# A decoder layer on one core: block 0's mixer rows beside the last projections, and four smaller moves

## The chip, the cores and the metric

One core of a Trainium2 chip. The time is that of the whole program on the device, in microseconds (us). Engines are named as in the profile: PE (tensor engine), DVE (VectorE), ACT (ScalarE), POOL (GpSimd), and SP, the queue that issues most DMAs. Each engine runs its instructions in order.

## The reference

One layer of a hybrid decoder over 2048 tokens of width 1024, one sequence, float32:

```
mod = silu(c) @ w_ada + b_ada            # shifts, scales, gates for both halves
h = rmsnorm(x, g_mix) * (1 + sc_m) + sh_m
q, k, v, f_logit, u = split(h @ w_in)    # 3 x 512, 8, 512 columns
attn = rmsnorm(forgetting_attention(q, k, v, log_sigmoid(f_logit + b)), g_attn_out)
ssm  = rmsnorm(s5_ssm(u, ...), g_ssm_out)            # 32 groups of 16 channels, 64 states
x = x + gt_m * (concat[attn, ssm] @ w_out)
h = rmsnorm(x, g_ffn) * (1 + sc_f) + sh_f
gate, val = split(h @ w_up)              # 2 x 2816 columns
y = (silu(causal_dwconv(gate, 3 taps)) * val) @ w_down
x = x + gt_f * y
out = rmsnorm(x, g_final)
```

The attention has 8 heads of 64; a score is q k / 8 plus the difference of two cumulated log gates, masked causally.

## The kernel before

**Tiles and precision.** Channels lie on the 128 partitions, tokens on the free axis; the 2048 tokens are 4 blocks of 512. Every large product is made of three matmuls in fp32r: operands are split into a high part (an ACT copy, names ending in `hi`) and the rest (a DVE subtraction, `lo`), and hi*hi, lo*hi and hi*lo are added in PSUM. A weight tile comes by DMA into `w_raw` (2 buffers) and is split into `w_hi` and `w_lo` (3 buffers each), in class `Weights`.

**Stages**, by the time of the profiled execution: to about 290 us loads, the modulation and the projection of u; to 611 the SSM, attention of block 0 and the q, k, v projections (those of blocks 2 and 3 last, they fill PE beside the SSM and attention(0)); to about 1935 the output projection and norm of block 0, attention of blocks 1 to 3 and, between its score tiles, the whole feed-forward part of blocks 0 and 1 (`up`, `down`); to 2387 the up products of blocks 2 and 3 taken in pairs (`up_pair`, 22 pairs of 19.5 us); to 2651 their down products (`down_pair`); then the last norm and the outputs.

**What sets the order.** The program is written as a list of operations; a scheduler places each engine's instructions by dependencies and priority. Code under `tc.high_priority()` goes ahead of what is written around it, `tc.issue_after(ins)` holds a DMA's place behind an instruction. A tile pool has tags with a number of buffers; a new tile of a tag waits until the readers of the tile that it replaces are done. A pool that is closed frees its memory, and later tiles at the same addresses wait in the same way.

**What the change touches.**
- `mix_t(b)` makes the operands of the output projection: it loads four row tiles of attention and SSM output (`row`, L1199 and L1200), squares the SSM half on ACT for its norm (L1202), scales it on DVE (L1208), transposes it with 16 PE transposes (L1212), scales and splits it (`yt`, `act_lo`, `act_hi`, channel tiles 4 to 7); the attention half needs its norm spread (L347) and gives channel tiles 0 to 3. `out_proj` (L1238) multiplies in the order 4, 5, 6, 7, 0, 1, 2, 3, 24 matmuls for each of 8 output tiles.
- `attention` finds row maxima of scores from augmented tiles `ka` (keys) and `qa` (queries) (L943, L948), then the scores again (L986, L987) with the maximum, the exponentials, and the products with v (L1007, L1011). Its score tiles come from `am_ps`: two PSUM banks of `att_ps` and two of a pool `sc_ps` that is opened after the projections. The augmented key tiles are three, then six.
- `ada_mid` sums a modulation gate (`tf`) on DVE beside the projections of blocks 2 and 3, from `wada` tiles that use the tags `ka3` and `ka4`; its accumulator `ada_mid` lies in the SSM's pool; the sum over partitions is a PE reading (L316).
- `finish(b)` is the last norm of block 0 or 1: token sums of squares on PE (L341), an inverse root on DVE, its spread (L347), 8 multiplications on DVE (L1311) and 8 output DMAs. For block 0 it stands at the end of that block's feed-forward part.
- `down_pair` keeps 8 output tiles in two halves of 4 PSUM accumulators; the 22 channel tiles `act` come back from DRAM in groups of 6, 6, 5 and 5 (`load_act`, one 512 KB DMA each); for each group, four weight tiles pass over it. In the last group of the last half (`cut`), two token halves p follow one another so that the first can be finished earlier; with 3 weight buffers the passes stand in the order d0 d1 d2 of p0, d0 d1 d2 of p1, then d3 of p0 and of p1. The `h` pool (9 high, 9 low tiles) holds the normed input of blocks 2 and 3 for `up_pair` and is closed before the down stage.

## Time and profile before

| | us |
|---|---|
| runs, median of three (range) | 2672.63 (2672.21 to 2674.73) |
| the profiled execution | 2669.64 |
| its span, first to last instruction | 2667.8 |
| PE busy in it | 2571.5 |
| DVE busy | 1928.8 |
| ACT busy | 1240.3 |
| POOL busy | 190.4 |
| mean granted PE clock | 0.973 |

"Busy" counts instructions of an engine on the span. A busy PE can still be slow: the granted clock says what share of its full clock it had. A window's line gives, for a stretch of the span, width, busy time and count for each engine, that clock, the DMA engines' busy share and their rate. A line of waits names who waited, for whom, the total, the number of times and the longest. In a timeline, the bracket at the end of a line holds the idle time of that engine just before, and what ended it.

### The profile page before, as it was taken

The numbers are of one execution on the slowest core, as the hardware profiler recorded it, in microseconds if no ns is written. First come the engines' busy times: TensorE is split into PE (matmuls) and PEld (weight loads), VectorE is DVE, ScalarE is ACT, GpSimd is POOL, SyncE is SP. The second block draws the span as 40 slices with busy tenths as digits, with TensorE's granted clock in tenths as the row PEclk, the third lists the DMA queues.
The fourth block names the chain that finished last, engine by engine and source line by source line (L and its number), as shares of the span: only waits on it lengthen the run. The fifth ranks groups of instructions, "written<-read, shape, count | busy, mean of one in ns | idle before, by whom it ended". The sixth has DMA issues, their size and how long they took to land. (4 is left out here: it accounts for less than half of the span.)

```text
span 2667.8 us, 35631 instructions
## 1 busy us (share of the span) xinstructions
PE 2571.5 (96%) x12343; PEld 2082.7 (78%) x12343; DVE 1928.8 (72%) x3568; ACT 1240.3 (46%) x2056; POOL 190.4 (7%) x146
## 2 busy tenths in 40 slices
...
GB/s 316 146 268 222 306 252 202 211 205 209 148 199 224 188 183 171 201 173 204 186 181 203 190 174 194 163 203 262 189 103 97 124 97 121 98 136 239 200 225 93
DMA packets 264196, 500.62 MB, mean 188 GB/s; under 512 B 26928, under 2 KB 111792, under 8 KB 264016
## 3 DMA queue, kind: packets, MB, share of 16 engines
...
q0 software_dynamic: 1280, 4.20, 0.4%
...
## 5 line engine op out<-in xcount | busy, mean ns | idle before, releaser
L78 DVE TENSOR_TENSOR w_lo<-w_raw,w_hi 128x1024 fp32r<-128x1024 f32 (+2 forms) x219 | 235.9, 1079 | 214.6 <-ACT w_hi L77 210.9
L77 ACT CAST w_hi<-w_raw 128x1024 fp32r<-128x1024 f32 (+2 forms) x219 | 203.3, 929 | 363.6 <-PE acc_ps L1481 100.9
L1264 PE MATMUL ff_ps<-h_lo,w_hi 128*128 128x512 f32 x704 | 279.3, 397 | 0.2 <-DVE h_lo L380 0.2
L1264 PE MATMUL ff_ps<-h_hi,w_lo 128*128 128x512 f32 x704 | 279.3, 397 | 0.0
L1264 PE MATMUL ff_ps<-h_hi,w_hi 128*128 128x512 f32 x704 | 279.2, 398 | 0.0
L996 ACT ACTIVATE pf<-sc_ps 128x512 f32<-128x512 f32 (+1 forms) x320 | 168.6, 542 | 165.3 <-PE sc_ps L987 84.6
L948 DVE TENSOR_REDUCE mx<-sc_ps 128x1 f32<-128x512 f32 (+2 forms) x320 | 195.8, 621 | 68.2 <-PE sc_ps L943 38.6
L998 DVE TENSOR_TENSOR pl<-pf,ph 128x512 fp32r<-128x512 f32 (+1 forms) x320 | 195.9, 620 | 29.5 <-ACT ph L997 28.8
L997 ACT CAST ph<-pf 128x512 fp32r<-128x512 f32 (+1 forms) x320 | 178.1, 568 | 81.7 <-PE o_ps L1007 78.4
L1006 DVE TENSOR_TENSOR acc<-acc,pf 128x512 f32<-128x512 f32 (+2 forms) x264 | 159.3, 606 | 22.6 <-ACT pf L996 19.4
L107 ACT CAST w_hi<-w_raw 128x1024 fp32r<-128x1024 f32 (+2 forms) x100 | 96.3, 963 | 142.9 <-PE ff_ps L1264 52.7
L1264 PEld LDWEIGHTS ff_ps<-h_lo,w_hi 128*128 128x128 f32 x704 | 132.9, 189 | 29.5 <-DVE h_lo L380 0.5
L1264 PEld LDWEIGHTS ff_ps<-h_hi,w_hi 128*128 128x128 f32 x704 | 133.1, 189 | 28.6
L1264 PEld LDWEIGHTS ff_ps<-h_hi,w_lo 128*128 128x128 f32 x704 | 132.9, 189 | 28.8
L1480 PE MATMUL acc_ps<-act,w_hi 128*128 128x512 f32 (+1 forms) x372 | 144.5, 389 | 10.6 <-DMA act<-act 6.5
L1481 PE MATMUL acc_ps<-act,w_hi 128*128 128x512 f32 (+1 forms) x372 | 143.9, 387 | 0.0
L1482 PE MATMUL acc_ps<-act,w_lo 128*128 128x512 f32 (+1 forms) x372 | 143.4, 387 | 0.2 <-DVE w_lo L78 0.2
L1296 PE MATMUL ff_ps<-act_hi,w_hi 128*128 128x512 f32 x352 | 140.0, 398 | 0.9 <-ACT rt L367 0.9
L1297 PE MATMUL ff_ps<-act_lo,w_hi 128*128 128x512 f32 x352 | 139.4, 397 | 0.0
L1298 PE MATMUL ff_ps<-act_hi,w_lo 128*128 128x512 f32 x352 | 139.0, 396 | 0.0
L986 PE MATMUL sc_ps<-qb,kb 128*128 128x512 f32 (+2 forms) x320 | 127.8, 400 | 2.3 <-DVE mx L948 1.3
L1007 PE MATMUL o_ps<-ph,vv 128*128 128x512 f32 (+1 forms) x320 | 122.2, 382 | 0.0
...
## 6 DMA issues: line engine op xcount, KB each, us to landing
...
```

Of the source, the lines that this page charges most:

```text
L77: nc.scalar.copy(hi[:, :n], raw[:, :n])
L78: nc.vector.tensor_tensor(out=lo[:, :n], in0=raw[:, :n], in1=hi[:, :n].bitcast(F32), op=ALU.subtract)
L948: V.reduce_max(out=mx[:, s, ch : ch + 1], in_=ps[:, 0:n], axis=AX.X)
L996: A.activation(pf[:, cs], ps[:, cs], AF.Exp)
L997: A.copy(ph[:, cs], pf[:, cs])
L998: V.tensor_tensor(out=pl[:, cs], in0=pf[:, cs], in1=ph[:, cs].bitcast(F32), op=ALU.subtract)
L1006: eng.tensor_tensor(out=acc[j][:, cs], in0=acc[j][:, cs], in1=pf[:, cs], op=ALU.add)
L1264: T.matmul(ps, lhsT=lt, rhs=rt, start=(n == 0), stop=(n == 23))
L1296: T.matmul(ps, lhsT=a, rhs=ah[:, ts], start=(c == 0), stop=False)
L1480: T.matmul(pss[d][:, ts], lhsT=a, rhs=ah, start=st, stop=False, skip_group_check=cut)
L1481: T.matmul(pss[d][:, ts], lhsT=a, rhs=al, start=False, stop=False, skip_group_check=cut)
L1482: T.matmul(pss[d][:, ts], lhsT=bb, rhs=ah, start=False, stop=sp_, skip_group_check=cut)
```

## The change

1. **Mixer rows.** The SSM's pools are closed after the SSM and attention(0); the feed-forward pools are opened there, and `mix_t(0)` is called, at high priority, ahead of the projections of blocks 2 and 3, with scratch tiles (`sq`) of the feed-forward pool. `out_proj(0)` stays behind the projections. For that the two score banks of `sc_ps` are replaced by the two banks that the projections used (`qs_last`, `vq_ps`), which stay open through attention; attention(0) runs with two `ka` tiles, and the tiles `ka2` to `ka4` and `kx0` are made after the projections.
2. **Gate accumulator.** `ada_mid` sums in a tile of tag `ka2`.
3. **finish(0)** is called in block 1, after the third `up` of its first group.
4. **First acts of the down stage.** Group 0 of `act` is loaded into tiles of the `h` pool (two 256 KB DMAs for each), which stays open to the end; the other act tiles have a buffer of their own each.
5. **The cut.** The last group's four weights are split into tiles of their own, so that all four passes of the first token half can go ahead of the second.

```diff
     vqp_ctx = ExitStack()
-    vq_psum = opened(vqp_ctx, "vq_ps", bufs=1, space=PSUM)
+    vq_psum = opened(vqp_ctx, "vq_ps", bufs=1, space=PSUM, side="right")
     in_ctx = ExitStack()
...
     def am_ps():
-        if sc_extra and next(am_n) % (2 + NSC) >= 2:
-            return sc_extra[-1].tile([P, 512], F32, name="sc_ps", tag="sc3", bufs=NSC)
+        n = next(am_n) % 4 if sc_extra else 0
+        if n >= 2:
+            return sc_extra[n - 2]()
         return att_ps.tile([P, 512], F32, name="sc_ps", tag="sc", bufs=2)
...
         for hf in range(2):
-            acc = pool.tile([P, TB], F32, name="ada_mid", tag="ada_mid", bufs=1)
+            acc = pool.tile([P, TB], F32, name="ada_mid", tag="ka2", bufs=1)
             for k in range(KT):
...
         return ts
-    qa_t, ka_all = itertools.cycle(aug_tiles(att_pool, "qa", 2)), aug_tiles(att_pool, "ka", 3)
+    qa_t, ka_all = itertools.cycle(aug_tiles(att_pool, "qa", 2)), aug_tiles(att_pool, "ka", 2)
     ka_t = [itertools.cycle(ka_all)]
     att_ps = opened(att_ctx, "att_ps", bufs=1, space=PSUM, side="right")
-    with tc.tile_pool(name="ssm", bufs=2) as sp, tc.tile_pool(name="ssm_ps", bufs=1, space=PSUM) as sps:
-        qs_ps = pair_ps(sps)
-        with tc.high_priority():
-            ssm(sp, sps)
-        attention((0,))
-        mid = itertools.chain(*(ada_mid(sp, sec, key) for sec, key in ((5, 'tf'),)))
-        for b in (2, 3):
-            h = []
-            for k in range(KT):
-                f = h_f()
-                Q.dma_start(f, f_d[b][k])
-                h.append(split_h(f, mod["sm"][:, k : k + 1]))
-            proj_qkv(b, h, qs_ps, each=mid)
-
-
-    cv = const.tile([P, NFF, 4], F32, name="cv")
-    Q.dma_start(cv, conv)
-    carry = const.tile([P, NFF, 2], F32, name="carry")
-    G.memset(carry, 0.0)
-    sc_extra.append(opened(att_ctx, "sc_ps", bufs=1, space=PSUM, side="right"))
+    qs_last_ps = opened(att_ctx, "qs_last", bufs=1, space=PSUM, side="right")
+    qs_ps = pair_ps(qs_last_ps)
+
+    def qs_last():
+        return qs_last_ps.tile([P, 512], F32, name="qs_ps", tag="qs", bufs=1)
+
+
+    yt = []
     ff_ctx, fp_ctx, rp_ctx = ExitStack(), ExitStack(), ExitStack()
-    vqp_ctx.close()
-    fps = opened(ff_ctx, "ffn_ps", bufs=2, space=PSUM)
-    row_pool = {"row": opened(rp_ctx, "rows", bufs=4)}
-    fp = opened(fp_ctx, "ffn", bufs=2)
-    actp = opened(fp_ctx, "act", bufs=6)
-    sq_pool.append(fp)
-    yt = []
-    ka_t.append(itertools.cycle(ka_all + aug_tiles(att_pool, "ka", 2, 3) + aug_tiles(fp, "kx", 1)))
     def ff_ps():
...
         ps_fn = ps_fn or ff_ps
+
+        def scratch():
+            return h_f() if b > 0 else fp.tile([P, TB], F32, name="sq", tag="sq", bufs=2)
         def parts(k):
...
             Q.dma_start(t[:, 1], ssm_d[b][s * P : (s + 1) * P, :])
-            junk = h_f()
+            junk = scratch()
             A.activation(junk, t[:, 1], AF.Square, accum_out=ss[:, s : s + 1])
...
                 T.transpose(ps[:, s * P : (s + 1) * P], rows[s][:, 1, k * P : (k + 1) * P], ident)
-            f = h_f()
+            f = scratch()
             A.activation(f, ps, AF.Copy, scale=gain[:, 20 + k : 21 + k])
...
             for c in range(c0, c0 + FFG[g]):
-                t = ap.tile([P, 2, TB], F32R, name="act", tag="act", bufs=NFF)
-                Q.dma_start(t.bitcast(F32), act_d[c][b % 2])
-                act.append(t)
+                if g == 0:
+                    act.append(h_parts())
+                    for j, t in enumerate(act[-1]):
+                        Q.dma_start(t.bitcast(F32), act_d[c][b % 2, :, j])
+                else:
+                    t = ap.tile([P, 2, TB], F32R, name="act", tag=f"act{c}", bufs=1)
+                    Q.dma_start(t.bitcast(F32), act_d[c][b % 2])
+                    act.append((t[:, 0], t[:, 1]))
         load_act(0)
...
                         if d not in ws:
-                            ws[d] = weights.get(*dn_slots[g][d])
+                            so, sn = dn_slots[g][d]
+                            own = [ap.tile([P, sn], F32R, name=f"w_{nm}", tag=f"cut_{nm}{d}", bufs=1)
+                                   for nm in ("hi", "lo")] if cut else (None, None)
+                            ws[d] = weights.split(weights.raw(so, sn), sn, *own)
                         wh, wl = ws[d]
...
                         for c in range(n):
-                            ah, al = act[c0 + c][:, 0, ts], act[c0 + c][:, 1, ts]
+                            ah, al = (t[:, ts] for t in act[c0 + c])
                             a, bb = wh[:, c * P : (c + 1) * P], wl[:, c * P : (c + 1) * P]
...
             Q.dma_start(out[b, d][:, ts], o)
+    with tc.tile_pool(name="ssm", bufs=2) as sp, tc.tile_pool(name="ssm_ps", bufs=1, space=PSUM) as sps:
+        with tc.high_priority():
+            ssm(sp, sps)
+    attention((0,))
+    cv = const.tile([P, NFF, 4], F32, name="cv")
+    Q.dma_start(cv, conv)
+    carry = const.tile([P, NFF, 2], F32, name="carry")
+    G.memset(carry, 0.0)
+    fps = opened(ff_ctx, "ffn_ps", bufs=2, space=PSUM)
+    row_pool = {"row": opened(rp_ctx, "rows", bufs=4)}
+    fp = opened(fp_ctx, "ffn", bufs=2)
+    actp = opened(fp_ctx, "act", bufs=6)
+    sq_pool.append(fp)
     with tc.high_priority():
-        x1, sq1 = out_proj(0, mix_t(0))
+        mt = mix_t(0)
+    mid = itertools.chain(*(ada_mid(att_pool, sec, key) for sec, key in ((5, 'tf'),)))
+    for b in (2, 3):
+        h = []
+        for k in range(KT):
+            f = h_f()
+            Q.dma_start(f, f_d[b][k])
+            h.append(split_h(f, mod["sm"][:, k : k + 1]))
+        proj_qkv(b, h, qs_ps, each=mid)
+    ka_t.append(itertools.cycle(ka_all + aug_tiles(att_pool, "ka", 3, 2) + aug_tiles(fp, "kx", 1)))
+    sc_extra += [qs_last, vq_ps]
+    with tc.high_priority():
+        x1, sq1 = out_proj(0, mt)
         yt += [y_tile(d, F32) for d in range(8)]
...
     att_ctx.close()
+    vqp_ctx.close()
     late_ctx, hh_ctx, up_ctx = ExitStack(), ExitStack(), ExitStack()
...
         for g, n in enumerate(FFG):
-            act = [up(h2, i + c) for c in range(n)]
+            act = []
+            for c in range(n):
+                act.append(up(h2, i + c))
+                if b == 1 and g == 0 and c == 2:
+                    finish(0, sq0)
             i += n
...
         if b == 0:
-            x1 = x1n
-            finish(b, sq)
+            x1, sq0 = x1n, sq
     first = up_pair(0, ops, ups)
...
     rp_ctx.close()
-    hp_ctx.close()
     with ExitStack() as stk:
...
             down_pair(b, ap, dps, misc, b == 3)
+    hp_ctx.close()
```

Lines after the edits above carry other numbers in the changed kernel: there L1196 is the transpose (L1212 before), L1222 out_proj (L1238), L944 the first score product (L943), L348 the spread (L347), L1248 and L1280 to L1282 up and down (L1264 and L1296 to L1298), L429 the projection (L428), L1434 and L1437 the act loads (L1448).

**PE at the start of out_proj(0).** Before, between the projections and the first matmul of out_proj: `row` transposes stand among the score products of block 1.

```order
L1212 MATMUL ff_ps<-ident,row 128x128 x6
L1007 MATMUL o_ps<-ph,vv 128x512
L1212 MATMUL ff_ps<-ident,row 128x128 x6
L986 MATMUL sc_ps<-qb,kb 128x512
L987 MATMUL sc_ps<-qa_3893,ka_3898 128x512
L1011 MATMUL o_ps<-pl,vv 128x512
L954 MATMUL sc_ps<-ident,mneg 4x128
L986 MATMUL sc_ps<-qb,kb 128x512
L987 MATMUL sc_ps<-qa_3893,ka_3898 128x512
L1212 MATMUL ff_ps<-ident,row 128x128 x4
L986 MATMUL sc_ps<-qb,kb 128x512
L347 MATMUL ff_ps<-ident,rs_y 128x128 x4
```

Of the changed kernel, the same transposes among the matmuls of a projection of block 3 (`qs_ps`, from `h` and `w`):

```order
L429 MATMUL qs_ps<-w_hi,h_lo 128x256
L429 MATMUL qs_ps<-w_hi,h_hi 128x256
L1196 MATMUL ff_ps<-ident,row 128x128 x3
L1008 MATMUL o_ps<-ph,vv 128x512
L1196 MATMUL ff_ps<-ident,row 128x128 x6
L1008 MATMUL o_ps<-ph,vv 128x384
L1196 MATMUL ff_ps<-ident,row 128x128 x3
L429 MATMUL qs_ps<-w_lo,h_hi 128x256
```

The end of the last projection there, and what follows it (`yt_5893` is channel tile 4 of block 0's mixer rows):

```order
L429 MATMUL vq_ps<-w_hi,h_lo 128x256
L944 MATMUL qs_ps<-ka_3897,qa_3893 128x384
L948 LDWEIGHTS identb
L948 MATMUL qs_ps<-mask_q,identb 128x128
L944 MATMUL qs_ps<-ka_3898,qa_3893 128x512
L944 MATMUL vq_ps<-ka_3897,qa_3893 128x512
L948 LDWEIGHTS identb
L948 MATMUL vq_ps<-mask_q,identb 128x128
L348 MATMUL ff_ps<-ident,rs_y 128x128
L1222 MATMUL ff_ps<-yt_5893,w_hi 128x512
L1222 MATMUL ff_ps<-act_lo,w_hi 128x512
```

The transposes have moved from behind the projections to the middle of them, and out_proj's first 24 matmuls follow the last projection after three short score products.

**SP around the end of the pair stage.** Before (`act18` to `act20` with `ah` and `al` are the last pairs' results on their way to DRAM, `act_...` the loads of group 0, `w_raw` 128x768 the down weights):

```order
L1431 DMA act18_174<-ah_22807 128x2x512
L1431 DMA act18_174<-al_22808 128x2x512
L69 DMA w_raw_23260<-in_w_flat 128x768
L1431 DMA act19_175<-ah_22946 128x2x512
L1431 DMA act19_175<-al_22947 128x2x512
L69 DMA w_raw_23284<-in_w_flat 128x768
L1431 DMA act20_176<-ah_23085 128x2x512
L1431 DMA act20_176<-al_23086 128x2x512
L69 DMA w_raw_23320<-in_w_flat 128x768
L69 DMA w_raw_23344<-in_w_flat 128x768
L69 DMA w_raw_23368<-in_w_flat 128x768
L1448 DMA act_23244<-act0_156 128x1024
```

And in the changed kernel (`h_hi` and `h_lo` are the halves of group 0's act tiles):

```order
L1415 DMA act19_175<-ah_22946 128x2x512
L1415 DMA act19_175<-al_22947 128x2x512
L69 DMA w_raw_23295<-in_w_flat 128x768
L1434 DMA h_lo_23248<-act1_157 128x512
L1434 DMA h_hi_23247<-act1_157 128x512
L1434 DMA h_lo_23252<-act2_158 128x512
```

and, eleven loads further on (those for block 3's first tiles are the last),

```order
L1434 DMA h_hi_24107<-act2_158 128x512
L1434 DMA h_lo_24108<-act2_158 128x512
L1415 DMA act20_176<-ah_23085 128x2x512
L1415 DMA act20_176<-al_23086 128x2x512
L69 DMA w_raw_23331<-in_w_flat 128x768
L69 DMA w_raw_23355<-in_w_flat 128x768
L69 DMA w_raw_23379<-in_w_flat 128x768
L69 DMA w_raw_23403<-in_w_flat 128x768
```

The loads of group 0 have moved ahead of the writes of `act20` and of the weights behind the second; in the changed kernel those of the other groups (not shown) follow four more weight loads.

**PE at the end of block 0's feed-forward part.** Before, the rows ahead of the first up product of block 1:

```order
L986 MATMUL sc_ps<-qb,kb 128x512
L987 MATMUL sc_ps<-qa_3893,ka_7139 128x512
L992 LDWEIGHTS identb
L992 MATMUL sc_ps<-mask_t,identb 128x128
L986 MATMUL sc_ps<-qb,kb 128x512
L987 MATMUL sc_ps<-qa_3893,kx_7142 128x512
L986 MATMUL sc_ps<-qb,kb 128x384
L987 MATMUL sc_ps<-qa_3893,ka_7139 128x384
L992 LDWEIGHTS identb
L992 MATMUL sc_ps<-mask_t,identb 128x128
L347 MATMUL ff_ps<-ident,rs_y 128x128 x4
L1264 MATMUL ff_ps<-h_hi,w_hi 128x512
```

Of the changed kernel, the last down products and the first up products:

```order
L1281 MATMUL ff_ps<-act_lo,w_hi 128x512
L1282 MATMUL ff_ps<-act_hi,w_lo 128x512
L1280 MATMUL ff_ps<-act_hi,w_hi 128x512
L1281 MATMUL ff_ps<-act_lo,w_hi 128x512
L1282 MATMUL ff_ps<-act_hi,w_lo 128x512
L944 MATMUL qs_ps<-ka_7272,qa_3894 128x512
L1248 MATMUL ff_ps<-h_hi,w_hi 128x512
L1248 MATMUL ff_ps<-h_lo,w_hi 128x512
L1248 MATMUL ff_ps<-h_hi,w_lo 128x512
L1248 MATMUL ff_ps<-h_hi,w_hi 128x512
L1248 MATMUL ff_ps<-h_lo,w_hi 128x512
L1248 MATMUL ff_ps<-h_hi,w_lo 128x512
```

The spread of finish(0) (L347) and the score products that stood between the last down and the first up are no longer there; one score product is.

## The prediction

> **What bounds the kernel now.** I read the page's busy table first, then windows of the tensor engine (PE) and its waits, then the timeline at each wait.
>
> ```profile
> span 2667.8 us, 35631 instructions
> PE 2571.5 (96%) x12343; PEld 2082.7 (78%) x12343; DVE 1928.8 (72%) x3568; ACT 1240.3 (46%) x2056; POOL 190.4 (7%) x146
> ```
>
> PE is busy 96% of the span, and the change takes no matmul away. So it can gain only where PE is idle or runs at a lower granted clock. The windows show those places (width, PE, PEld, DVE, ACT and POOL busy, granted clock, DMA share, GB/s):
>
> ```profile
> 572.00:605.00 33.00, 33.00 (x244) 31.11 (x244) 17.82 (x32) 12.77 (x23) 0.00 (x0) 1.00 0.82 256
> 605.00:615.00 10.00, 6.87 (x36) 5.64 (x34) 6.32 (x10) 3.10 (x5) 0.52 (x1) 0.83 0.74 253
> 615.00:625.00 10.00, 8.20 (x26) 5.30 (x26) 7.62 (x16) 0.96 (x3) 0.98 (x2) 0.50 1.02 344
> 625.00:635.00 10.00, 6.79 (x21) 5.04 (x22) 6.23 (x29) 5.67 (x15) 0.00 (x0) 0.50 0.35 114
> 635.00:645.00 10.00, 8.28 (x49) 6.41 (x48) 9.85 (x24) 8.39 (x16) 0.00 (x0) 0.97 0.33 106
> 690.00:712.00 22.00, 20.54 (x80) 15.33 (x79) 18.89 (x44) 11.86 (x21) 0.00 (x0) 0.69 0.46 146
> 697.00:710.00 13.00, 12.90 (x46) 9.65 (x46) 11.47 (x33) 6.26 (x11) 0.00 (x0) 0.50 0.40 118
> 712.00:1270.00 558.00, 557.72 (x2582) 446.61 (x2582) 452.54 (x808) 302.96 (x509) 0.00 (x0) 1.00 0.58 189
> 1270.00:1325.00 55.00, 49.69 (x208) 37.66 (x207) 49.96 (x105) 29.32 (x50) 0.00 (x0) 0.84 0.47 156
> 1280.00:1292.00 12.00, 10.53 (x31) 6.12 (x31) 9.92 (x24) 4.41 (x9) 0.00 (x0) 0.72 0.45 140
> 1305.00:1322.00 17.00, 13.15 (x59) 10.64 (x58) 14.79 (x36) 9.07 (x16) 0.00 (x0) 0.70 0.44 152
> 2385.00:2397.00 12.00, 5.52 (x19) 4.14 (x18) 8.88 (x10) 4.66 (x5) 0.00 (x0) 0.72 0.61 208
> 2396.00:2410.00 14.00, 14.00 (x59) 11.23 (x59) 2.12 (x3) 1.57 (x2) 0.00 (x0) 0.97 0.91 326
> 2410.00:2424.00 14.00, 10.94 (x46) 8.19 (x44) 0.96 (x1) 1.07 (x2) 0.00 (x0) 1.00 1.03 408
> 2420.00:2431.00 11.00, 7.45 (x20) 5.26 (x19) 2.74 (x3) 2.40 (x3) 0.00 (x0) 0.69 0.86 296
> ```
>
> I count as lost: width less PE busy times clock. From 605 to 645 that is 10 - 6.87 x 0.83 = 4.3, then 5.9, 6.6 and 2.0: **18.8 us**. The stretch at 690 loses 7.8; the two inside the change from block 0 to block 1, 4.4 and 7.8; the start of the down stage 8.0, and a later place in it 5.9. The long stretches between lose almost nothing: 0.28 us of 558 idle.
>
> **The change, part by part.**
>
> *A: block 0's mixer rows beside the projections.* These rows stand behind the 18.8 us (waits: total, times, longest; tile: durations in ns, first and last start):
>
> ```profile
> PE sc_ps L987 <- DMA qa<-rrow: 5.1, 2, 3.8
> PE sc_ps L316 <- DVE ada_mid L1102: 1.6, 1, 1.6
> 617.71 0.33 SPq L1199 DMA_DIRECT2D row<-att  x1
> 623.40 0.63 ACT L1202 ACTIVATE h_f<-row 128x512 f32<-128x512 f32 x1 [10.00 <-DMA row<-ssm]
> L1212 PE MATMUL ff_ps<-ident,row x16: 270/272/273, 636.0 to 639.8; 128*128 128x128 f32 x16
> ```
>
> Now the row loads are issued only after the projections; ScalarE sits 10.0 us until they land, its squares lead to the scaling and to 16 transposes (636.0 to 639.8), and out_proj can start only then. In the changed order the loads, four squares, transposes and splits lie among the projections of block 3, where PE is fully busy at clock 1.00, VectorE has 33 - 17.8 = 15 us free and ScalarE 20 us; the work moved is some 5 us on each (16 transposes of 0.27 at most on PE, 4.3; 4 squares of 0.63 on ScalarE and the copies). That is hidden as long as it doesn't hold the projections' own evictions. Behind the projections PE then finds 24 out_proj matmuls ready, and more between the first score tiles.
>
> What is new there, none of it in the trace: (1) the row loads follow block 0's SSM and attention writes on SP, and the squares wait for them with the evictions of block 3's q, k and v queued behind on ScalarE. Bounds: 0 and the 10.0 us that the same squares waited; I take 1.5, since PE has a whole projection group queued. (2) ka2 now holds the gate accumulator, so its memset (POOL), its loads and the third key tile's score matmul wait for the accumulator's last reading, 15 out_proj matmuls ahead on PE. Bounds: 0 and the 3.8 us of the load wait on L987; I take 1.5. The reading itself waits for late loads of w_ada, as now (1.6). (3) The attention half of the rows still comes late, after attention(0)'s last head: 0 to 1.6 again, I take 1.0. Idle: 4.0 us. A short idle also costs clock:
>
> ```profile
> 694.81 0.50 PE L986 MATMUL sc_ps<-qb,kb 128*128 128x512 f32 x1 [1.26 <-DVE mx L948]
> ```
>
> After this wait of 1.26 us the clock granted is 0.50 from 697 to 710, which costs 12.90 x 0.5 = 6.5 us. I charge the three waits together 4 us for it (two in three of such a stretch). Left: 8.0 of 18.8, so **A gains 10.8** (bounds -3, with the waits at their upper ends, 15.4, and a whole slow stretch of 6.5, and 18.8).
>
> The Trainium skill ("TensorE: Matmul & The Clock Gate", section "HAM oscillation — how this bites in real kernels") says that PE must not idle for more than about 3.4 us if it is to keep its clock; by it, waits of 1 to 1.5 us would cost only themselves, and A's gain would be 14.8. The row above is against it: a gap of 1.26 us, and half the clock soon after.
>
> *B: the stretch at 690* is the norm chain from out_proj(0) to h2. The change shifts which score tiles fill it but not the chain: **0** (bounds -6.5, one more slow stretch, to 7.8).
>
> *C: finish(0) behind the third up of block 1.*
>
> ```profile
> PE sc_ps L1042 <- ACT sums L1039: 2.5, 1, 2.5
> 1322.49 4.06 DVE L1311 SCALAR_TENSOR_TENSOR yt<-yt,gain,rt 128x512 f32<-128x512 f32 x6
> ```
>
> Before, PE passes from the last down through two token sums, a head's end and the spread of finish(0) before the first up; VectorE is 91% busy there (49.96 of 55). After, ups follow the last down directly, two of them taken channel tile by channel tile as h2 gets ready, and the 8 multiplications of finish(0) (4.06 for 6, so 5.4) come some 30 us later beside ups, where VectorE has 19% free. The loss of 7.8 should largely go; that of 4.4 comes before the place and stays. **C gains 6** (bounds -4.4, a second gap like the first, to 12.2).
>
> *E: the down stage's first act tiles.*
>
> ```profile
> 2369.00:2387.00 18.00, 18.00 (x79) 14.56 (x78) 11.02 (x14) 7.88 (x11) 0.00 (x0) 1.00 0.31 103
> 2373.14 0.39 PE L1387 MATMUL up_y<-h_hi,w_lo 128*128 128x512 f32 x1
> 2389.13 0.33 SPq L69 DMA_DIRECT2D w_raw<-in_w_flat  x1
> 2389.50 17.04 SPq L1448 DMA_DIRECT2D act<-act  x12
> 2393.96 0.76 PE L1480 MATMUL acc_ps<-act,w_hi 128*128 128x512 f32 x1 [6.48 <-DMA act<-act]
> 2396.33 0.37 ACTq L1431 DMA_DIRECT2D act<-al  x1
> 2423.77 0.83 ACT L77 CAST w_hi<-w_raw 128x768 fp32r<-128x768 f32 x1 [7.70 <-DMA w_raw<-in_w_flat]
> 2424.65 0.80 PE L1480 MATMUL acc_ps<-act,w_hi 128*128 128x512 f32 x1 [3.55 <-ACT w_hi L77]
> ```
>
> Before, the act loads follow a weight load that isn't issued before 2389.1, and PE waits 6.48 us. After, group 0 goes into h tiles, whose last reading by the last pair starts at 2373.14, and SP issues these loads ahead of act20's writes and the next weights. 4.2 MB are to land in the 14 us until PE needs them at 2387.5, in a stretch whose DMA engines are 0.31 busy: the 8.0 go. The second wait stays. Group 1's third pass of weights stands on SP behind all 11 act loads of groups 1 and 2, and the third of these takes the memory of the al tile, whose write is issued at 2396.33. With 5.7 us to land (what the row loads took from 617.71 to 623.40) that is 2402; 9 acts of 0.524 MB and 0.39 MB of weights at 408 GB/s take 12.5 us, and the cast and its neighbours 1.0: 2415.5. PE has 6 passes of 18 matmuls to do from 2387.5, at 14.00 / 59 = 0.237 us each (2396 to 2410), and is there at 2413.1. That is a wait of 2.4 us; with the 326 GB/s of the window before it would be 5.6; I take 4, the middle, and 2.3 of clock as before (5.9 - 3.55). So 6.3 is lost there instead of 5.9, and 8.0 + 5.9 - 6.3 = 7.6; I take **7 for E**, since the later end of that wait (5.6 and more) weighs on one side only (bounds 3, with 326 GB/s and a landing 3 us later, to 13.9). Splitting acts into halves issues 10 more loads on SP per block, hidden by the same free stretch; block 3's come early too.
>
> *F: the end, two token halves in weights of their own.*
>
> ```profile
> 2648.80 0.38 PE L1480 MATMUL acc_ps<-act,w_hi 128*128 128x256 f32 x1 [0.58 <-DVE yt L1440]
> 2650.70 0.50 PE L341 MATMUL misc_ps<-ones,sq_acc 128*128 128x1 f32 x4
> 2651.90 0.42 DVE L333 TENSOR_TENSOR sq_acc<-sq_acc,sq 128x256 f32<-128x256 f32 x1
> 2654.30 0.45 PE L347 MATMUL misc_ps<-ident,rs_y 128*128 128x128 f32 x1 [3.10 <-DVE rs_y L176]
> 2656.66 8.90 SPq L1526 DMA_DIRECT2D out_y<-yt  x16
> 2660.11 0.66 PE L347 MATMUL misc_ps<-ident,rs_y 128*128 128x128 f32 x2 [4.40 <-DVE rs_y L176]
> ```
>
> Before, both halves end together: the first half's chain (2650.7 to 2654.3) runs ahead of the second's, whose spread comes at 2660.11, and 16 outputs leave in one queue. After, the first half's sums stand 26 matmuls before the end. The second's chain then takes what the first's takes now: its last squares are summed at 2651.90 + 0.42 = 2652.3, and 3.6 later comes the spread, 2655.9 against 2660.1: 4.2, and 0.58 of the wait at 2648.8. Against it, four multiplications of the first half stay ahead of it on VectorE; I charge 0.8. **F gains 4** (bounds 2 to 5.5).
>
> *Rest.* Score banks stay four, key tiles six; attention(0) with two key tiles instead of three stands beside projections that leave PE no idle: 0, within 2 either way.
>
> **Sum.** 10.8 + 0 + 6 + 7 + 4 = 27.8. The profiled execution took 2669.64 (1.84 around its span), so 2641.8; the median shown, 2672.63, is 3.0 above that execution: **2645**.
>
> **Rivals.**
> - *More goes than I think.* The al write lands earlier and no second wait is left at the start of the down stage (6.3), and both gaps of C go (6): 2633. For it: DMA is free before 2387; against: the late weights are last on the queue in any case.
> - *A is eaten.* The squares wait for rows as long as they do now (10.0), hold the evictions, and PE idles and slows among the projections instead: A about 0, 2656. For: SP is in order and DMA already 0.82 busy in 572 to 605.
> - *Short gaps leave the clock alone*: A loses only its 4 of idle, 2641. Against: the row at 694.81. The Trainium skill's page "TensorE: Matmul & The Clock Gate" would make this the rule.
> - *E doesn't do what it says.* The early loads hold SP for tiles not yet free, so act20's writes and the weights behind come late, and PE waits as long as now: 2652.
> - *Slower: VectorE becomes the bound in new stretches.* Where it was 91% busy (1270 to 1325), PE lost 12.2 us in 55; at 81% (712 to 1270) next to nothing. The new order moves every head's place against the ups. From 27.8 / 12.2 = 2.3 new such stretches on, the gain is gone; at three, 36.6 lost: 2681. Against: VectorE's work in sum is the same.
>
> **How the numbers follow.** My forecast (2638 to 2651) 0.43; more goes 0.12; A eaten 0.20, of which 0.03 together with E at nothing and so within 0.2% of before (5.3 us, about what a measurement of this kernel can tell from no change); clock left alone 0.08; E at nothing 0.07; slower stretches 0.10, of which 0.02 end within 0.2%. Faster 0.87, same 0.05, slower 0.08. The range 2630 to 2661 takes in all but the last rival and the worst of A.
>
> **What would show it.** Right: PE busy at clock 1.00 through 605 to 620 with out_proj matmuls, no wait of the squares over 3 us; ups right behind the last down of block 0; no act wait at the first down pass, a wait of about 4 us for weights after the sixth down pass; the last spread about 5 us behind the last matmul instead of 9. Wrong: a projection stage longer than now, waits on ka2 or on mx in new places, VectorE over 90% in stretches that now run at 81%.

## The result, and the profile after

The changed kernel takes 2651.97 us (median of 4 runs, 2648.09 to 2656.42) beside 2673.24 for the kernel before on the same chip: a ratio of 0.9921, interval 0.9903 to 0.9938, so 21 us less. In a second group of runs it took 2651.5 beside 2672.53 (0.9926, 0.9913 to 0.9939). The forecast was 2645 with a range of 2630 to 2661; the direction was right, and 7 of the 28 us that the sum promised did not come. The time is in the range, and a microsecond above the 2638 to 2651 of the forecast's own course.

The profiled execution's span is 2648.8 us instead of 2667.8, that is 19.0 less. Its busy table:

```profile
span 2648.8 us, 35639 instructions
PE 2555.7 (96%) x12343; PEld 2069.9 (78%) x12343; DVE 1924.3 (73%) x3568; ACT 1238.4 (47%) x2056; POOL 190.8 (7%) x146
```

The same 12343 matmuls; PE is busy 15.8 us less, which is matmuls at a higher clock (mean granted clock 0.983 instead of 0.973), and idle some 3 us less.

**Marks in time.** Some work is done by both kernels in the same order, so its start times show where the 19.0 us came from, without any clock. These are PE's matmuls of the pair stage (first `up_x`, last `up_x` product) and of the down stage (last `acc_ps` product); of each group the durations in ns (shortest, median, longest) and the first and last start. Before, then after:

```profile
L1387 PE MATMUL up_x<-h_hi,w_hi x88: 390/396/497, 1934.2 to 2369.9; 128*128 128x512 f32 x88
L1387 PE MATMUL up_x<-hh,w_lo x176: 390/394/628, 1953.2 to 2387.1; 128*128 128x512 f32 x176
L1480 PE MATMUL acc_ps<-act,w_hi x372: 281/392/796, 2394.0 to 2650.3; 128*128 128x512 f32 x166, 128*128 128x256 f32 x20
```

```profile
L1371 PE MATMUL up_x<-h_hi,w_hi x88: 390/395/503, 1923.5 to 2359.1; 128*128 128x512 f32 x88
L1371 PE MATMUL up_x<-hh,w_lo x176: 390/394/632, 1942.2 to 2376.4; 128*128 128x512 f32 x176
L1472 PE MATMUL acc_ps<-act,w_hi x276: 280/392/628, 2393.3 to 2633.7; 128*128 128x512 f32 x118, 128*128 128x256 f32 x20
```

The pair stage begins 10.7 us earlier (1934.2 to 1923.5) and ends as much earlier (2387.1 to 2376.4): nothing changed in it. From its last product to the down stage's last, 263.2 became 257.3: 5.9 for the loads of the first acts (E). (All nine profiles that have E, and not the edit of weights_first, take 256.9 to 259.2 there.) From there to the end of the span, 17.5 became 15.1: 2.4 for the cut (F). The 10.7 are A, B, C and the rest together, for which the forecast had 16.8.

**By stage.** What PE loses (width less busy time times clock) shows where these 10.7 lie. The columns are width, then busy time and count of PE, PEld, DVE, ACT and POOL, the granted clock, the DMA share and GB/s. Before, the stages at 612 (out_proj(0)), 1250 (from block 0 to block 1) and 2370 (start of the down stage), and the same of the changed kernel:

```profile
612.00:660.00 48.00, 39.92 (x169) 29.20 (x168) 39.76 (x96) 24.47 (x48) 1.50 (x3) 0.79 0.52 177
1250.00:1345.00 95.00, 89.69 (x390) 69.56 (x389) 82.88 (x163) 50.69 (x87) 0.00 (x0) 0.91 0.54 176
2370.00:2440.00 70.00, 59.81 (x238) 46.87 (x236) 24.39 (x27) 16.45 (x21) 0.00 (x0) 0.90 0.72 263
```

```profile
612.00:660.00 48.00, 44.04 (x194) 35.50 (x194) 30.60 (x60) 12.49 (x18) 1.56 (x3) 0.86 0.64 218
1250.00:1345.00 95.00, 91.85 (x415) 72.77 (x414) 84.63 (x169) 55.90 (x94) 0.00 (x0) 0.98 0.59 200
2370.00:2440.00 70.00, 63.31 (x262) 49.46 (x261) 22.10 (x26) 16.04 (x20) 0.00 (x0) 0.98 0.69 248
```

From 612 to 660, 48 - 39.92 x 0.79 = 16.5 became 48 - 44.04 x 0.86 = 10.1; from 1250 to 1345, 13.4 became 5.0; from 2370 to 2440, 16.2 became 8.0. Summed from windows of 10 us, where the rounded clock does less harm, the whole table is as below (also for the later kernels; the names are explained with the experiments). Span less loss is 2520 to 2527 us in every row, so these losses follow the span to within some 3 us.

| loss of PE, us | 0-290 | 290-560 | 560-660 | 660-720 | 720-1250 | 1250-1340 | 1340-1900 | 2360-2440 | span |
|---|---|---|---|---|---|---|---|---|---|
| before | 47.4 | 7.9 | 18.8 | 8.0 | 0.3 | 12.8 | 1.4 | 14.7 | 2667.8 |
| after | 48.2 | 10.2 | 11.8 | 6.9 | 0.0 | 4.4 | 2.8 | 8.3 | 2648.8 |
| after, again | 44.9 | 11.3 | 13.5 | 6.6 | 0.0 | 4.5 | 2.8 | 8.3 | 2645.8 |
| mix_late | 49.0 | 11.1 | 9.8 | 7.5 | 0.1 | 4.2 | 2.7 | 7.8 | 2646.2 |
| finish_back | 49.5 | 9.5 | 13.0 | 7.1 | 0.0 | 14.7 | 1.6 | 8.5 | 2657.4 |
| act_ring | 47.9 | 11.4 | 14.9 | 6.9 | 0.0 | 3.9 | 3.6 | 11.8 | 2655.4 |
| cut_shared | 48.3 | 11.4 | 12.4 | 6.4 | 0.0 | 4.4 | 2.8 | 8.7 | 2651.3 |
| no_rows | 48.8 | 10.1 | 19.0 | 5.8 | 0.5 | 4.4 | 3.5 | 9.8 | 2658.0 |
| rows_behind | 48.3 | 17.1 | 8.4 | 10.2 | 0.3 | 4.3 | 3.2 | 8.2 | 2654.5 |
| weights_first | 46.8 | 14.8 | 9.3 | 8.9 | 0.0 | 3.2 | 2.8 | 5.1 | 2648.0 |
| loaded_late | 49.4 | 10.2 | 25.3 | 9.8 | 5.1 | 5.0 | 6.5 | 7.6 | 2676.9 |
| attention_behind | 49.9 | 10.3 | 15.3 | 12.0 | 4.9 | 4.6 | 4.9 | 8.6 | 2671.1 |
| both | 48.9 | 11.9 | 10.0 | 14.2 | 3.2 | 4.2 | 3.3 | 2.5 | 2657.4 |
| gate_early | 45.5 | 16.5 | 11.6 | 14.4 | 1.1 | 5.0 | 5.7 | 2.6 | 2661.5 |

**A, read closely.** The mixer rows did go beside the projections. ACT's first square and the 16 transposes (durations and first and last start) of the changed kernel, then two steps of DVE (the first and the last of the root of block 0's attention norm) and PE behind the last projection, with the idle time before each instruction in brackets, and windows of that place:

```profile
582.74 0.63 ACT L1186 ACTIVATE sq<-row 128x512 f32<-128x512 f32 x1 [3.56 <-DMA row<-ssm]
L1196 PE MATMUL ff_ps<-ident,row x16: 270/272/273, 592.9 to 598.3; 128*128 128x128 f32 x16
```

```profile
613.94 0.17 DVE L166 TENSOR_SCALAR rs_v<-ss_att 128x4 f32<-128x4 f32 x1
623.13 0.16 DVE L176 SCALAR_TENSOR_TENSOR rs_y<-rs_t,rs_y 128x4 f32<-128x4 f32 x1
621.07 0.79 PE L944 MATMUL qs_ps<-ka,qa 66*128 66x512 f32 x1 [2.31 <-DVE mx L949]
622.61 0.80 PE L944 MATMUL vq_ps<-ka,qa 66*128 66x512 f32 x1 [0.75 <-DVE vst L490]
623.35 0.47 PE L348 MATMUL ff_ps<-ident,rs_y 128*128 128x128 f32 x1
623.47 0.77 PE L1222 MATMUL ff_ps<-yt,w_hi 128*128 128x512 f32 x1
```

```profile
612.00:618.00 6.00, 5.86 (x36) 5.65 (x36) 3.28 (x16) 1.79 (x3) 0.00 (x0) 0.72 0.54 166
618.00:621.00 3.00, 0.77 (x7) 0.53 (x5) 3.00 (x6) 1.32 (x2) 0.00 (x0) 1.00 0.66 232
621.00:628.00 7.00, 6.18 (x15) 4.40 (x16) 3.86 (x9) 0.00 (x0) 0.00 (x0) 0.51 0.90 296
634.00:642.00 8.00, 8.00 (x33) 6.32 (x32) 6.33 (x13) 2.37 (x4) 0.28 (x1) 0.79 0.59 194
```

The squares run at 582.7 instead of behind the projections, and the transposes at 592.9 to 598.3 instead of 636.0; out_proj starts at 623.5 instead of 642.5. What is left of the loss: DVE is full from 618 to 621 (3.00 of 3.00: gate sums, a weight split, then the maxima), so PE waits 2.31 us for the maxima that free the first score bank; and then it runs at clock 0.51 from 621 to 628. These two windows lose 2.2 and 3.8, a second slow stretch from 634 to 642 another 1.7, and one ahead of them, from 612 to 618, 1.8: 9.5 of the 10.1. That first one has no wait close ahead of it (the last, of 0.83 us, ended at 605.5), and PE is busy 5.86 of 6.00 us. What stands ahead of its slow matmuls (614.3 to 617.6) is 16 matmuls of one column each, 2.0 us of them (L342 and L317). Of the whole 48 us, 4.0 are idle (48 - 44.04) and 6.2 slow clock (44.04 x 0.14).

The wait for the maxima is not all that holds out_proj. PE takes its matmuls in order, and the first of the spread (L348, at 623.35) stands ahead of out_proj's first product (623.47). It needs the root of the attention norm, whose steps on DVE begin at 613.94 and end at 623.29, with five gate sums (one after a wait of 1.11 us for its load) and two weight splits between them. So out_proj, whose first products need only the SSM half, could not begin before 623.3, whatever the maxima did.

The Trainium skill ("TensorE: Matmul & The Clock Gate", section "HAM oscillation — how this bites in real kernels") names gaps above about 3.4 us as those that cost clock. The longest gap here is 2.31 us, and the clock is halved behind it: the rows are against that rule, as the one at 694.81 was. The same page (section "What's actually happening") has a window of about 3.4 us in which activity is watched, whatever its start. By the durations of single matmuls PE is slow from 614.3 to 617.6, from 621.1 to 627.8 and from 634.7 to 638.1, that is for 3.3, 6.7 and 3.4 us, which agrees with it, and so does PE's 0.77 busy of 3.00 us before the second of them. Which share of activity keeps the clock, and whether it was the 16 small matmuls that lost it at 614.3, no run here shows.

**E, read closely.** SP and PE at the start of the down stage of the changed kernel (first the loads of group 0 into h tiles, later those of the other groups):

```profile
2354.90 0.33 SPq L1434 DMA_DIRECT2D h_lo<-act  x1
2388.60 8.89 SPq L1437 DMA_DIRECT2D act<-act  x11
2398.50 1.62 SPq L69 DMA_DIRECT2D w_raw<-in_w_flat  x2
```

```profile
2376.58 0.39 PE L1472 MATMUL acc_ps<-h_hi,w_hi 128*128 128x512 f32 x1
2395.92 0.51 PE L1472 MATMUL acc_ps<-act,w_hi 128*128 128x512 f32 x1 [1.72 <-DMA act<-act]
2409.36 0.55 PE L1472 MATMUL acc_ps<-act,w_hi 128*128 128x512 f32 x1 [4.57 <-ACT w_hi L77]
```

The first down product starts at 2376.58 without a wait, 0.2 us behind the last of the pairs; the wait of 6.48 is gone. The second wait is 4.57 (4 was taken, from 2.4 to 5.6), at the place that was forecast: the weights at 2398.50 stand behind 11 act loads. A wait of 1.72 for the first act of group 1 was not in the forecast.

**F, read closely.** The last 15 us of the changed kernel:

```profile
2633.98 0.28 PE L1474 MATMUL acc_ps<-act,w_lo 128*128 128x256 f32 x1
2635.20 0.40 PE L348 MATMUL misc_ps<-ident,rs_y 128*128 128x128 f32 x2 [0.93 <-DVE rs_y L176]
2636.04 1.66 DVE L1516 SCALAR_TENSOR_TENSOR yt<-yt,gain,misc_ps 128x256 f32<-128x256 f32 x4 [0.35 <-ACT rt L1509]
2636.09 2.77 POOL L1514 TENSOR_TENSOR yt<-yt,rt 128x256 f32<-128x256 f32 x4 [291.76 <-ACT rt L1509]
2638.24 0.65 DVE L169 TENSOR_SCALAR rs_i<-rs_i 128x2 int32<-128x2 int32 x1
2640.79 0.66 PE L348 MATMUL misc_ps<-ident,rs_y 128*128 128x128 f32 x2 [4.37 <-DVE rs_y L176]
```

The first half's spread comes 1.2 us behind the last matmul and the second's 6.8 behind (from start to start, where before it was 9.5; about 5 was forecast). The first half's multiplications, four on DVE (1.66 us) and four on POOL (2.77), lie in the middle of the second half's chain, and a step of that chain takes 0.65 us beside them.

### The profile page after: what moved, and what is told of

Read it like the earlier page. It is cut to its first block, busy times and chain, and to the rows that moved or that the text cites. A ratio compares the mean times of both kernels' runs of the same rounds, so it can differ in the third digit from the quotient of the medians.

```text
span 2648.8 us, 35639 instructions
## 1 busy us (share of the span) xinstructions
PE 2555.7 (96%) x12343; PEld 2069.9 (78%) x12343; DVE 1924.3 (73%) x3568; ACT 1238.4 (47%) x2056; POOL 190.8 (7%) x146
## 3 DMA queue, kind: packets, MB, share of 16 engines
q0 software_dynamic: 1280, 4.20, 0.4%
## 5 line engine op out<-in xcount | busy, mean ns | idle before, releaser
L1248 PE MATMUL ff_ps<-h_lo,w_hi 128*128 128x512 f32 x704 | 279.8, 397 | 0.8 <-DVE h_lo L381 0.8
L1248 PE MATMUL ff_ps<-h_hi,w_lo 128*128 128x512 f32 x704 | 280.3, 398 | 0.0
L1248 PE MATMUL ff_ps<-h_hi,w_hi 128*128 128x512 f32 x704 | 279.5, 399 | 0.0
L999 DVE TENSOR_TENSOR pl<-pf,ph 128x512 fp32r<-128x512 f32 (+1 forms) x320 | 195.3, 620 | 18.7 <-ACT ph L998 17.5
L997 ACT ACTIVATE pf<-sc_ps 128x512 f32<-128x512 f32 (+2 forms) x184 | 98.4, 539 | 124.9 <-PE sc_ps L988 74.1
L1248 PEld LDWEIGHTS ff_ps<-h_lo,w_hi 128*128 128x128 f32 x704 | 133.5, 190 | 29.6 <-DVE h_lo L381 1.1
L1248 PEld LDWEIGHTS ff_ps<-h_hi,w_lo 128*128 128x128 f32 x704 | 133.4, 189 | 29.0
L1248 PEld LDWEIGHTS ff_ps<-h_hi,w_hi 128*128 128x128 f32 x704 | 133.3, 190 | 28.7 <-issue 0.2
L1280 PE MATMUL ff_ps<-act_hi,w_hi 128*128 128x512 f32 x352 | 139.3, 398 | 0.2 <-ACT rt L368 0.2
L1282 PE MATMUL ff_ps<-act_hi,w_lo 128*128 128x512 f32 x352 | 139.3, 397 | 0.0
L949 DVE TENSOR_REDUCE mx<-sc_ps 128x1 f32<-128x512 f32 (+2 forms) x164 | 97.7, 600 | 49.6 <-PE sc_ps L944 24.5
L1371 PE MATMUL up_x<-hh,w_hi 128*128 128x512 f32 x352 | 113.4, 401 | 7.8 <-DVE hh L378 6.0
L1012 PE MATMUL o_ps<-pl,vv 128*128 128x512 f32 (+2 forms) x312 | 116.0, 374 | 0.9 <-DVE pl L999 0.9
L1371 PE MATMUL up_z<-hh,w_hi 128*128 128x512 f32 x352 | 111.7, 398 | 1.4 <-ACT vz L1387 1.4
L1472 PE MATMUL acc_ps<-act,w_hi 128*128 128x512 f32 (+1 forms) x276 | 105.4, 382 | 6.7 <-ACT w_hi L77 4.6
```

The lines of the kernel that those rows point to most:

```text
L999: V.tensor_tensor(out=pl[:, cs], in0=pf[:, cs], in1=ph[:, cs].bitcast(F32), op=ALU.subtract)
L1248: T.matmul(ps, lhsT=lt, rhs=rt, start=(n == 0), stop=(n == 23))
L1280: T.matmul(ps, lhsT=a, rhs=ah[:, ts], start=(c == 0), stop=False)
L1282: mark[0] = T.matmul(ps, lhsT=bb, rhs=ah[:, ts], start=False, stop=(c == n - 1))
L1371: mark[0] = T.matmul(ps, lhsT=lt, rhs=rt, start=(first and n == 0), stop=(n == 11), skip_group_check=not first)
L1472: T.matmul(pss[d][:, ts], lhsT=a, rhs=ah, start=st, stop=False, skip_group_check=cut)
```

## The experiments

Each kernel is the changed kernel with the edit shown, except no_rows, which is the kernel before with C, E and F. The time is the median; the ratio is to the kernel before, timed in the same group. Runs of one group have the same time in the last column.

| kernel | us | ratio (interval) | before, same group |
|---|---|---|---|
| mix_late | 2650.22 | 0.9935 (0.9917 to 0.9954) | 2670.26 |
| finish_back | 2661.09 | 0.9966 (0.9954 to 0.9977) | 2670.26 |
| act_ring | 2656.82 | 0.9946 (0.9934 to 0.9958) | 2670.26 |
| cut_shared | 2653.05 | 0.9933 (0.9922 to 0.9944) | 2670.26 |
| after, again | 2651.50 | 0.9926 (0.9913 to 0.9939) | 2672.53 |
| no_rows | 2659.73 | 0.9952 (0.9940 to 0.9964) | 2672.53 |
| rows_behind | 2652.11 | 0.9924 (0.9912 to 0.9936) | 2672.53 |
| weights_first | 2648.87 | 0.9912 (0.9899 to 0.9926) | 2672.53 |
| loaded_late | 2679.00 | 1.0026 (1.0014 to 1.0038) | 2672.16 |
| attention_behind | 2672.79 | 0.9991 (0.9979 to 1.0004) | 2672.16 |
| both | 2668.30 | 0.9981 (0.9967 to 0.9994) | 2672.16 |
| gate_early | 2667.57 | 0.9981 (0.9968 to 0.9994) | 2672.62 |

### mix_late: mix_t(0) called behind the projections

```diff
-    with tc.high_priority():
-        mt = mix_t(0)
     mid = itertools.chain(*(ada_mid(att_pool, sec, key) for sec, key in ((5, 'tf'),)))
...
     with tc.high_priority():
-        x1, sq1 = out_proj(0, mt)
+        x1, sq1 = out_proj(0, mix_t(0))
```

> Edit: only the call of mix_t(0) goes back behind the projections; pools, banks and the other moves stay. Parts add up (theory): the stage from 560 to 712 us loses again what it lost before, 26.8 instead of 18.7 us, and the time is 8 us above the changed kernel: about 2660. Rival, the rows pay nothing because new waits eat them: within 2 us of the changed kernel, 2652, and the loss moves into the projections. Rival, the rows' early place also shifts the heads so that the passage from block 0 to block 1 is smooth: 8 + 8 us, about 2668, and the stage at 1270 to 1345 loses about 12 again.

The transposes run at 596.0 to 601.5, still among the projections: pools and priorities place the rows, not the line on which they are written. Behind the projections PE's order is another one: all four matmuls of the spread stand together, and out_proj's products run without score products between, from 625.9 to 671.6 (in the changed kernel from 623.5 to 676.0, with score products between). The time is 2650.22, and the ratio, 0.9935, can't be told from the changed kernel's 0.9921 and 0.9926. So this run undid nothing of A, and it stands for the changed kernel in its group.

### finish_back: finish(0) at the end of block 0 again (C undone)

```diff
-                if b == 1 and g == 0 and c == 2:
-                    finish(0, sq0)
...
-            x1, sq0 = x1n, sq
+            x1 = x1n
+            finish(b, sq)
```

> Edit: only finish(0) goes back to the end of block 0. Theory, the spread and the token sums of finish(0) stood between the last down and the first up: the passage loses about 12 us instead of 4, and the time is about 8 us above the changed kernel, 2660. Rival, the gain there came from another alignment of the heads (from the other moves) and finish(0) costs nothing: within 2 us of 2652, with the passage still at about 4 us lost.

10.9 us over mix_late, with intervals of some 4 us each (10.7 by the ratios of this run and of the changed kernel, 0.9966 and 0.9926). The stage from 1250 to 1345, and the longest of PE's waits in it (total, times, longest):

```profile
1250.00:1345.00 95.00, 88.22 (x375) 68.22 (x375) 82.34 (x166) 53.84 (x90) 0.00 (x0) 0.89 0.54 178
PE sc_ps L944 <- DMA qa<-qb: 2.9, 1, 2.9
```

It loses 95 - 88.22 x 0.89 = 16.5, where the changed kernel loses 5.0, and the other stages are as in the changed kernel. The longest wait is for a load of queries of the next head, not for finish(0)'s own spread; in the changed kernel the longest PE wait of that stage is 1.7 (on `ph`). So finish(0) seems to cost by what it holds up: with it back, PE has no up products to go on with while a head begins. This is read from the order; no run separates it.

### act_ring: the old ring of act tiles (E undone)

```diff
-                if g == 0:
-                    act.append(h_parts())
-                    for j, t in enumerate(act[-1]):
-                        Q.dma_start(t.bitcast(F32), act_d[c][b % 2, :, j])
-                else:
-                    t = ap.tile([P, 2, TB], F32R, name="act", tag=f"act{c}", bufs=1)
...
+                t = ap.tile([P, 2, TB], F32R, name="act", tag="act", bufs=NFF)
...
     rp_ctx.close()
+    hp_ctx.close()
```

> Edit: only group 0 of the down stage goes back into the act ring, and the h pool is closed before. Theory: the first wait of the down stage for act tiles (6.5 us before, none now) and its slow clock are back, the second for weights shrinks to 3.5 from 4.6: 6 us above the changed kernel, 2658. Rival, the wait for the late weights only moves: within 2 us of 2652.

6.6 us over mix_late. PE's waits at the start of its down stage:

```profile
2386.37 0.79 PE L1467 MATMUL acc_ps<-act,w_hi 128*128 128x512 f32 x1 [6.16 <-DMA act<-act]
2416.15 0.50 PE L1467 MATMUL acc_ps<-act,w_hi 128*128 128x512 f32 x1 [2.95 <-ACT w_hi L77]
```

The first wait is back (6.16, before 6.48). By the marks (last `up_x` product 2379.8, last `acc_ps` product 2640.7) the stage takes 260.9 beside 257.3: 3.6 of the 5.9 between the two kernels. The other 2.3 are not explained by this edit.

### cut_shared: the cut's weights in the shared buffers (F undone)

```diff
-                                   for nm in ("hi", "lo")] if cut else (None, None)
+                                   for nm in ("hi", "lo")] if False else (None, None)
```

> Edit: only the weights of the cut go back to the shared three buffers, so the passes are interleaved again. Theory: the last spread comes 9 us behind the last matmul instead of about 6, 2.7 us above the changed kernel: 2655. Rival, the 16 outputs on one queue (9.7 us for them) set the end in both: within 1 us of 2652.

2.8 us over mix_late, which the intervals don't tell from nothing. The marks do: from the last `acc_ps` product to the end 17.2, as before (17.5), where eight other profiles, all with the cut (after, again, mix_late, finish_back, act_ring, no_rows, rows_behind, weights_first), have 14.7 to 15.5. F is worth 2.1 to 2.4.

### no_rows: the kernel before with C, E and F (A undone)

> Edit: the kernel before with the moves of finish(0), of the act loads and of the cut, and nothing else; pools, score banks, key tiles and mixer rows as before. (Calling mix_t(0) late, alone, left PE's order as in the changed kernel: the scheduler puts the rows among the projections as soon as the pools allow.) Theory, pools of their own pay 8 us from 560 to 720: this one loses 26 there and takes 2660. Rival, the pools pay nothing: 2652. Rival, the smooth passage between the blocks needs them too: 2668, with 12 us lost from 1250 to 1345.

8.2 us over the changed kernel in its group. The stage and its longest PE wait:

```profile
612.00:660.00 48.00, 38.23 (x172) 27.56 (x171) 38.99 (x94) 23.14 (x46) 1.50 (x3) 0.79 0.59 198
PE sc_ps L987 <- DMA qa<-rrow: 5.9, 2, 4.6
```

It loses 17.8 there as before (16.5), and the rows come late as before; the stage from 1250 loses 4.4, as in the changed kernel, so C doesn't need A. The pair stage begins at 1931.6. In five profiles of kernels that are the changed one up to there (after, again, act_ring, cut_shared, weights_first) it begins at 1921.1 to 1926.9, mean 1924.1: A, here the first two moves together, is worth 7.5 by this mark, give or take 3.

Counted from the kernel before, it looks otherwise: with A and without C (finish_back, 1931.7) the pair stage begins 2.5 us earlier than in the kernel before (1934.2), with C and without A (no_rows) 2.6, and with both 10.1. Either each of the two needs the other, or the one profile of before, whose execution is 3 us below its median, begins early; this is not settled.

### rows_behind: the transposes behind the last projection

```diff
-    with tc.high_priority():
-        mt = mix_t(0)
...
     sc_extra += [qs_last, vq_ps]
+    with behind():
+        mt = mix_t(0)
```

> Edit: all pools and the rest as changed, but mix_t(0) is held behind the last projection matmul, so its loads, squares and 16 transposes come between the projections and out_proj. Theory, what pays is that out_proj finds its operands ready: the loss from 612 to 660 goes from 10 back to 15 or more, the loss from 560 to 612 (2.0) goes to about 1, time 2657 to 2660. Rival, it pays that the pools come earlier, whatever the rows do: 2652.

Here `behind()` holds the work behind the last projection's matmul. The loads of the SSM half and the squares stayed early (583 to 592); the transposes moved:

```profile
L1196 PE MATMUL ff_ps<-ident,row x16: 272/273/415, 622.7 to 625.3; 128*128 128x128 f32 x16
612.00:660.00 48.00, 44.26 (x226) 37.15 (x225) 31.50 (x58) 17.67 (x27) 1.56 (x3) 0.93 0.76 263
```

2652.11 beside 2651.50: the place of the transposes on PE pays nothing. The stage even loses less (48 - 44.26 x 0.93 = 6.8), and the next one more (10.2 for 6.9): 3 us go from one to the other. (The 17.1 from 290 to 560 lies ahead of the place that the edit changes; weights_first, which is the changed kernel up to the down stage, has 14.8 there.)

### loaded_late: the row loads too behind the projections

```diff
-                Q.dma_start(v_d[b][s, :, cc * 4 : cc * 4 + 4], vst.bitcast(F32))
+                stored[0] = Q.dma_start(v_d[b][s, :, cc * 4 : cc * 4 + 4], vst.bitcast(F32))
...
-    with tc.high_priority():
-        mt = mix_t(0)
...
     sc_extra += [qs_last, vq_ps]
+    with tc.high_priority(), tc.issue_after(stored[0].ins):
+        mt = mix_t(0)
```

> Edit: pools, banks and the other moves as changed, but the loads of block 0's mixer rows are held on SP behind the last store of v, so that loads, squares, transposes and all that follow come after the projections, as before the change. (With only the transposes held back, the time was 2652.1 beside 2651.5.) Theory, what pays is the time of the loads and the squares, since ScalarE then doesn't sit until rows land: the loss from 612 to 660 us goes from 10 to 15 or more and the time to about 2659. Rival, the pools and score banks pay by themselves: 2652, loss near 10.

2679.0, 7 us slower than the kernel before. DVE's wait for the squares and PE's longest wait in that stage:

```profile
632.39 0.17 DVE L166 TENSOR_SCALAR rs_v<-ss 128x4 f32<-128x4 f32 x1 [7.96 <-ACT sq L1186]
PE sc_ps L317 <- DVE ada_mid L1103: 12.9, 1, 12.9
```

SP issues the eight row loads at 620.3 to 626.2 and the gate's last `wada` loads only behind them, so the gate's reading on PE waits 12.9 us, and the heads behind it come later. The expectation had priced only the squares' wait. With rows_behind this points to the time of the loads, not of the transposes, as what A gains by. But this run also moved the gate, so it is no clean measure, and that the earlier pools and the other score banks pay a part by themselves is not ruled out.

### weights_first: the act loads of groups 2 and 3 behind the fourth weight load

```diff
-                        if half == 0 and d == ds[1] and not last:
+                        if half == 0 and d == ds[3 if g else 1] and not last:
                             with tc.issue_after(weights.last.ins):
```

> Edit: the act loads of groups 2 and 3 of the down stage follow the fourth weight load of the group before instead of the second, so that group 1's third weights stand ahead of group 2's acts on SP. Theory, the wait of 4.6 us for w_hi in the changed kernel is those weights behind 11 act loads: it goes, and with its slow clock 5 to 6 us, 2646. Rival, the act loads of group 2 or the weights themselves then come late: the wait moves to the next group, 2652.

PE's waits in its down stage:

```profile
PE acc_ps L1472 <- ACT w_hi L77: 2.1, 1, 2.1
PE acc_ps L1472 <- DMA act<-act: 1.4, 3, 0.7
```

The wait of 4.57 at 2409 is gone, as the queue read from the trace said, and the stage from 2360 loses 5.1 for 8.3. From the last pair product to the last `acc_ps` product it takes 255.2 beside 257.3. 2648.87 is the lowest median of all; the 2.6 us under the changed kernel lie within the intervals, and the marks, 2.1, agree with them. The wait of 2.1 that is left is one for later weights (2415.8). In both and gate_early, which hold the same edit, the stretch takes only 251.9 and 252.3, and their longest such wait is 0.7 and 1.5: the edit is worth 2 to 5 us, and why it gave least here is open.

### attention_behind, and both

The theory: PE's wait for the maxima (2.31 at 621) is the cause of the slow clock, and goes when heads of blocks 1 to 3 start only behind out_proj's first tile. `both` adds the edit of weights_first.

```diff
+            if b == 0 and d == 0:
+                first_d[0] = mark[0]
...
-    attention((1, 2, 3), LEAD)
+    with tc.issue_after(first_d[0].ins):
+        attention((1, 2, 3), LEAD)
```

> Edit: attention of blocks 1 to 3 is held behind the first output tile of out_proj(0), so that its first score products don't stand on PE between the last projection and out_proj. Theory, the wait of 2.3 us (3.7 in another run) of the third score product for its bank's maximum, with the slow clock after it, is most of the 10 us still lost from 612 to 660: it goes to 5 or less, time 2646 to 2648. Rival, the heads start later, so the filling for the norm chain near 690 or for the passage between the blocks is missing: the loss from 660 to 720 or from 1250 to 1345 grows by as much, 2652.

> Edit: the weights of the down stage ahead of the later act loads, as in the run before (2648.9 beside 2651.5 for the changed kernel), together with attention held behind out_proj's first tile. If both gains stand in their own stages they add: 2.6 + 4 us, about 2645. If holding attention back pays nothing: 2649.

It failed: 2672.79, no gain over before at all, and 2668.30. At the place, and in the next stage of attention_behind:

```profile
625.83 0.47 PE L348 MATMUL ff_ps<-ident,rs_y 128*128 128x128 f32 x1 [5.75 <-DVE rs_y L176]
660.00:720.00 60.00, 53.55 (x219) 38.80 (x219) 46.91 (x95) 27.66 (x47) 0.00 (x0) 0.89 0.48 159
```

The wait for the maxima was filling a longer one: without score products PE waits 5.75 us for the root of the attention half's norm, which the spread needs and whose steps on DVE run from 616.87 to 625.77, again with gate sums and weight splits between. The heads then come later than the norm chain that they used to fill: 660 to 720 loses 12.0 for 6.9, and 720 to 1900 loses 3 to 7 us more in these two kernels than in the changed kernel. The profile of `both` is of one of its fastest executions (2659.1, of 2657.6 to 2677.0), so its losses explain only a part of its median.

### gate_early: the gate's second half without the wait for the first

```diff
-            acc = pool.tile([P, TB], F32, name="ada_mid", tag="ka2", bufs=1)
+            acc = pool.tile([P, TB], F32, name="ada_mid", tag=f"ka{2 + 2 * hf}", bufs=1)
             for k in range(KT):
-                wt = att_pool.tile([P, TB], F32, name="wada", tag=f"ka{3 + k % 2}", bufs=1)
+                wt = att_pool.tile([P, TB], F32, name="wada", tag="ka3", bufs=1)
```

(with the edit of weights_first)

> Edit: on top of the weights ahead of the later act loads (2648.9, 0.9912 of before), the second half of the gate has an accumulator of its own (tag ka4, with one buffer ka3 for the w_ada tiles), so that it needn't wait for PE's reading of the first half. In the changed kernel 6 of its 8 sums run on VectorE from 615 to 632.6, each waiting for a load of w_ada, with the maxima of scores, the spread of block 0's attention norm and ka2 behind them; when attention was held back instead, the wait for that spread was 5.75 us. Theory, this is most of the 10 us that the changed kernel still loses from 612 to 660: it falls to 5 or less, and the time to 2643 to 2645, 0.990 of before. Rival, the sums now go to the stage before 560, where VectorE is full, and cost there, or the heads stand in other places: 2649 or more.

The gate's sums left the place, and it loses as much as in the changed kernel. Its windows around it:

```profile
618.00:624.00 6.00, 3.81 (x17) 2.14 (x16) 5.73 (x10) 2.46 (x4) 0.00 (x0) 0.77 0.91 302
624.00:634.00 10.00, 9.95 (x38) 8.86 (x38) 3.59 (x18) 0.00 (x0) 1.03 (x2) 0.50 0.46 166
```

PE's waits there are all below 1 us now, and still it is busy only 3.81 of 6 and then has half the clock for 10 us, though it is busy 9.95 of them (24 of these matmuls have one column, 5.4 us). The steps of the attention norm's root take 2.5 us without the gate sums between (626.27 to 628.79) instead of 9.3, but they begin 12 us later, since attention(0) ends later: its token sums on PE are at 624.17 instead of 611.33. Out_proj begins at 629.98, behind the spread's first matmul at 629.91. The stage from 290 loses 16.5 for 10.2, which one `wada` buffer need not have caused, as weights_first and rows_behind have 14.8 and 17.1 there; 660 to 720 loses 14.4. The time is 2667.57: taking the gate's sums away did not make out_proj's start fast.

## Why the prediction was right or wrong

**A (10.8 forecast, 7 to 8 measured).** The mechanism was right: no_rows is 8.2 us slower, and the stage from 560 to 660 loses 11.8 for 18.8 (9.3 to 14.9 in the other profiles of that order). The step that was mis-sized is the clock: 4 us of idle and 4 of slow clock were to stay, and from 612 to 660 it is 4.0 and 6.2. The idle is right in sum and not in place. The squares waited 3.56 at 582.7 and held nothing that PE needed, and among PE's waits from 600 to 660 none is for `ka2`; the largest was not on the list, PE on the maxima of the first score tile, while DVE takes gate sums and splits first (2.31). The forecast had out_proj's matmuls ready behind the projections and the attention half late, for 1.0 us, behind them; in PE's order the spread of that half stands ahead of them, and its root is done at 623.29, 5 us behind the last projection. By the rival "short gaps leave the clock alone" the clock would have cost nothing, and 621 to 628 at 0.51 is against that; by the rival "A is eaten" nothing would have come, and 582.7 and 592.9 are against that: the rows got in among the projections, where PE is idle 2.0 us of 52 (560 to 612). The last projection is pushed from 611.8 to 618.2; from 560 up to there PE loses 3.8 us where it lost 3.0, so most of the push is work.

**B (0).** 8.0 became 6.9, and 6.4 to 8.9 in the other profiles of the changed order: no gain is shown, as forecast.

**C (6 forecast, 8 to 11 measured: 8.4 by the stage, 7.6 by the start of the pair stage, 10.9 by the runs).** Two windows of 10 us of the changed kernel, the first where the kernel before had its gap of 4.4, the second where finish(0) now stands:

```profile
1280.00:1290.00 10.00, 10.00 (x45) 8.04 (x44) 10.00 (x19) 6.33 (x12) 0.00 (x0) 1.00 0.58 197
1330.00:1340.00 10.00, 7.28 (x26) 5.40 (x26) 9.42 (x25) 4.17 (x8) 0.00 (x0) 0.83 0.67 227
```

The forecast let 4.4 stay at 1280 and took 7.8 as largely gone. Of the 12.8 the whole stage now loses 4.4, but in another place: at 1280 up products keep PE at 10.00 of 10.00, with DVE full too, and 4.0 go from 1330 to 1340 (10 - 7.28 x 0.83), where nothing was charged. There PE waits for a head's probabilities while finish(0)'s chain runs:

```profile
1333.73 0.49 PE L1008 MATMUL o_ps<-ph,vv 128*128 128x512 f32 x1 [1.68 <-ACT ph L998]
1334.34 1.02 PE L348 MATMUL ff_ps<-ident,rs_y 128*128 128x128 f32 x4
1336.16 2.74 DVE L1295 SCALAR_TENSOR_TENSOR yt<-yt,gain,rt 128x512 f32<-128x512 f32 x4
```

The spread is at 1334.34 and the multiplications, whose cover the forecast argued, come only behind the gap. In no_rows, where finish(0) has the same place in the code, it is as forecast: 4.4 stay from 1280 to 1300, and nothing else is lost. So the step that fell is the place of what stays; whether finish(0)'s chain makes the new gap was not tried. A full DVE alone made no gap at 1280.

**E (7 forecast, 5.9 by the marks).** First wait gone, second 4.57 where 4 was taken, and 1.72 more for an act of group 1. The second wait's place and cause were right: with the weights ahead of the act loads, in weights_first, the 4.57 go, a wait of 2.1 for later weights stays, and the stage gains 2 us (5 in the two other kernels with that edit). What was not charged is the 1.72, of the same crowd of loads. By the runs alone E is 6.6, but act_ring's marks give back only 3.6 of the 5.9, and no_rows, which has E, takes 259.2 there, 4.0 less than before.

**F (4 forecast, 2.4 by the marks).** The second half's chain was taken to last as long as the first's did before (3.6 us) plus 0.8. From the end of its last squares (2635.70) to the spread at 2640.79 it took 5.1: 1.66 us of DVE's multiplications ahead of it, and steps that stretch beside POOL's. So 0.7 of the 1.6 that are missing are this chain; 0.3 are the way from that spread to the end (8.0 for 7.7), and 0.6 the wait at 2648.8, which was counted here and lies ahead of the mark.

**The rest (0, within 2).** Here 4 to 5 us went that no term held: 290 to 560 loses 9.5 to 14.8 in the seven profiles of the changed order (after, again, mix_late, finish_back, act_ring, cut_shared, weights_first), for 7.9 in the one profile of before and 10.1 in no_rows, and 1340 to 1900 loses 2.8 for 1.4. Whether attention(0) with two key tiles costs 2 us there, or the one profile of before is a low one, is not settled; no_rows, which has three key tiles, speaks for the second.

**Sum.** By the marks 10.7 + 5.9 + 2.4 = 19.0, where the forecast had 16.8 + 7 + 4 = 27.8. The forecast stood 6.1 us too high before the pair stage, 1.1 in the down stage and 1.6 at the end. Of the first, little lies in A, B and C: the stages from 560 to 1340, which hold them, lose 16.8 less (7.0, 1.1, 0.3 and 8.4), just what was forecast for them, though A came short and C gave more, which is luck. The larger part is the rest, that was put at nothing. The pieces undone one by one give 8.2 + 10.9 + 6.6 + 2.8 = 28.5, more than the 21 us of the whole; with some 4 us of uncertainty in each, and marks that give 7.5, 7.6, 3.6 and 2.1, so 20.8, the difference is not shown to be more than scatter.

**Its own signs.** Of what was to show it right, the ups behind the last down (but for one score product), the first down pass without a wait for acts and the later wait of about 4 us for weights came. The squares' wait of at most 3 us (3.56), the last spread 5 us behind the last matmul (6.8) and out_proj from 605 at full clock (623.5, and 0.72 from 612 to 618) did not. Of what was to show it wrong, a longer projection stage and a wait for maxima in a new place came. That the time is also that of the rival "E doesn't do what it says", 2652, is chance: the first wait for acts, which that rival keeps, is gone.

**The rival of DVE as the bound in new stretches** didn't come in the changed kernel (720 to 1250 loses 0.0). But what it described, heads that fall differently against the ups and the norm chain, did come in three experiments: loaded_late, attention_behind and gate_early moved work at 620 and took 16 to 27 us more than the changed kernel, a part of it lost hundreds of us later. What keeps the remaining 10 us at 612 to 660 is open: attention_behind and gate_early removed the waits that they named, and others took their place. In the changed kernel and in both of these, out_proj begins within 0.13 us of the spread's first matmul; a kernel that takes the spread behind out_proj's first products was not run.
